# Moving the scale and bias of eight layer norms from GpSimd to VectorE in a five-layer float32 network

## The chip, the cores and the metric

The kernel runs on one core of a Trainium2 chip. The metric is the device time of one execution in microseconds; the time shown is the median of a few runs. The engines named below are TensorE (PE, with its weight loads as PEld), VectorE (DVE), ScalarE (ACT), GpSimd (POOL) and the DMA queue of SyncE (SP).

## The reference

The input is one sequence of 512 tokens with 1024 features, in float32. It passes through four layers of a first block and one layer of a second. Each layer of the first block is, with a mixer that is differential attention (layers 0 and 3), a gated linear recurrence (1) or window attention (2):

```
h = layer_norm(ALPHA * h + mixer(h), ln_g[i, 0], ln_b[i, 0])
u = square(relu(h @ w_up[i])) @ w_down[i]
h = layer_norm(ALPHA * h + u, ln_g[i, 1], ln_b[i, 1])
h = h + sigmoid(h @ w_ple_gate[i]) * (p[i] @ w_ple[i])

layer_norm(x, g, b) = (x - mean) * rsqrt(var + 1e-5) * g + b     # over the 1024 features
```

So there are eight layer norms, two for each of four layers. The second block has two RMS norms, a mixer and a gated feed-forward part, and a last RMS norm ends the network; the change doesn't touch them.

## The kernel before

The residual `hres` stays on the chip as four token tiles of 128 tokens by 1024 features. Beside it lies its transpose, by feature, as two float32 parts `hTh` and `hTl` (the rounded value and what is left), since every product is made as three passes over such parts (`mm3`, lines 274 to 276: high by high, low by high, high by low). Weights come from memory in halves of 512 KB into three buffers `raw`; ScalarE rounds a half into `wh` (L133), and VectorE subtracts to get `wl` (L134), after which that `raw` buffer is free for the next transfer. There are three buffers each of `wh` and `wl`.

Around each layer norm stands a `boundary`: the last products of the phase before are made token tile by token tile (`tail`), and as soon as two token tiles are complete, the work for that half of the tokens follows. VectorE adds the product bank to `hres` (L584), takes the statistics (L532 to L534) and the inverse root (L343 to L359), and the tile is normalized, one tile of each half by ScalarE (L541) and one by VectorE (L537). Then `transposed` runs over the half in four steps of two feature chunks: TensorE transposes four blocks into a bank (L489), ScalarE applies scale and bias by feature into a scratch tile `e` (L501), VectorE casts it into `hTh` (L507) and subtracts for `hTl` (L508). The products of the next phase read `hTh` and `hTl`.

The residual itself needs the same scale and bias, now along the free axis. They are loaded once for each norm, spread over all partitions, into one buffer `gb` of the pool `a8` (it appears as `a` in the rows). Before the change GpSimd does this in place on each token tile: one multiplication (L546) and one addition (L547) of 128x1024. The readers of the scaled residual come later: after the first norm of a layer it is the first addition in `down` (L586), after two quarters of the feed-forward width have been projected; after the second norm it is `add` in `gate` (L724, L726), once the four banks `acc` of the gate's first half are complete.

After the first norm `ffn` projects three weight tiles by halves of the tokens (`fm` with `split=True`): first all three tiles for tokens 0 to 255, then all three for 256 to 511, so that the second half may come late. Two banks (`psA`) alternate; `evict` empties one by ScalarE (L668), VectorE (L669), ScalarE (L333), VectorE (L334). After the second norm the products of `ple` (which don't need the norm) and then those of `gate` follow, in four banks `psD`.

The order of each engine's queue is set at compile time by a planner: it follows the order in which the program names the instructions, and fills an engine that it believes to be idle with later work that is ready by its own estimate. Each queue is then executed in that order. Only inside the attention and recurrence parts is the order written by hand.

Of the kernel before, what the change touches and what calls it, by code (L numbers as in the profile page):

```python
# [21 lines left out]
NT = S // P  # L22
D = 1024
# [25 lines left out]
def shape_constants():  # L49
    """Arrays that depend on the shapes alone."""  # L50
# [45 lines left out]
def weave(main, fill, rate):  # L96
    """Emit the steps of main with those of fill between them, rate of fill per unit that main yields."""
    due = 0.0
    for n in main:
        due += rate * (1 if n is None else n)  # L100
        while due >= 1:
            due -= 1
            next(fill, None)
    run(fill)


class Weights:
    """A weight tile [128, k, n or 2048 / k], to be loaded as its exact parts hi + lo, by halves of k.

    src: (halves, k, n, perm); halves[z]: [(slice of columns, source [128, k / 2, columns])];  # L110
    perm: how the columns are reordered on the way, as (destination view, source view).
    """
# [24 lines left out]
class Stream:  # L137
    """Jobs (sources, steps of the loaded weight tiles), in order, and the sources of a tail; loaded ahead."""
# [15 lines left out]
    def convert(self, n):  # L154
        """The first n halves, with as many more on their way as there is room for."""
        self.fetch(self.converted + self.RAW)
        for t, z in self.halves[self.converted:n]:
            t.convert(z)
            self.converted += 1
            self.fetch(self.converted + self.RAW)  # L160
# [23 lines left out]
class Net:  # L184
# [18 lines left out]
    # ---------------------------------------------------------------- helpers  # L203
# [31 lines left out]
    def dma2(self, out, in_):  # L235
        """Small loads, out of the way of the weights."""
        self.nc.gpsimd.dma_start(out=out, in_=in_)
# [10 lines left out]
    def cols(self, w, c0):  # L248
        """256 columns of a [1024, n] matrix: [128, 8, 256]."""
        wv = w[:, c0:c0 + 256].rearrange("(k p) n -> p k n", p=P)  # L250
        return [[(self.ALL, wv[:, 4 * z:4 * z + 4])] for z in range(2)], 8, 256, None

    def rows4(self, w, r0, n):
        """512 rows, 512 columns: [128, 4, 512]."""
        wv = w[r0:r0 + 512, n * 512:n * 512 + 512].rearrange("(k p) n -> p k n", p=P)
        return [[(self.ALL, wv[:, 2 * z:2 * z + 2])] for z in range(2)], 4, 512, None

    def rows2(self, w, c0, c1):
        """Two chunks of 128 rows, 1024 columns: [128, 2, 1024]."""
        return [[(self.ALL, w[c * P:c * P + P].rearrange("(k p) n -> p k n", p=P))] for c in (c0, c1)], 2, 1024, None  # L260
# [17 lines left out]
    def mm3s(self, products):  # L278
        """Independent products of the same kind, pass by pass: those on other rows of the array may overlap."""
        mm = self.nc.tensor.matmul  # L280
        for n in range(3):
            for ps, (lh, ll), (rh, rl) in products:
                mm(ps, ll if n == 2 else lh, rl if n == 1 else rh, start=n == 0, stop=n == 2)
# [4 lines left out]
    def fm_steps(self, tiles, evict, split=False, act=None):  # L288
        """Feature-major products: evict(tile index, block, psum [128 features, tokens c], c).

        split: by halves of the tokens, over all the tiles, so that the second half may come late.
        """
# [25 lines left out]
    def tm256_steps(self, w, evict):  # L318
        """Token-major products of a [1024, 256] weight tile: evict(pair of token tiles, psum [128, 2, 256])."""
# [11 lines left out]
    def split_to(self, hi, lo, src):  # L331
        """src (f32) into hi + lo."""
# [3 lines left out]
    def rsqrt(self, v, n, engine=None):  # L336
        """1/sqrt of positive [128, n] values: a first guess from the exponent, a Newton and a Halley step."""
# [24 lines left out]
    def exp_small(self, out, x):  # L362
        """exp(x) = ((1 + tanh(x/16)) / (1 - tanh(x/16)))**8 of a small tile."""
# [11 lines left out]
    # ---------------------------------------------------------------- setup  # L375
# [8 lines left out]
    def columns(self, name, rows):  # L384
        """Vectors as columns: rows of 128 values, transposed on TensorE."""
# [14 lines left out]
    def lambdas(self):  # L400
        """lambda of the differential attention, negated."""
# [17 lines left out]
    def tables(self):  # L419
# [16 lines left out]
        # halved biases and scales of the sigmoids taken as tanh  # L436
# [9 lines left out]
        # sinks, negated and not  # L446
# [4 lines left out]
    def biases(self):  # L451
        """The bias of every relative position by head, reversed and laid out as Toeplitz blocks."""
# [25 lines left out]
    # ---------------------------------------------------------------- norms  # L478
    def transposed(self, src, half, scale=None, bias=None):
        """hT of the two token tiles of a half: x * scale + bias by feature, split."""  # L480
        nc = self.nc
        hs = slice(half * 256, half * 256 + 256)
        for cp in range(NC // 2):
# [22 lines left out]
            if bias is not None:  # L506
                nc.vector.tensor_copy(hi, f)  # L507
                nc.vector.tensor_sub(lo, f, hi.bitcast(F32))  # L508

    def boundary(self, tail, half):  # L510
        """The last products of a phase, by token tile, and what follows each half of the tokens."""
# [5 lines left out]
    def layer_norm(self, tail, i, n):  # L517
        """hres <- LN(hres), hT of it."""
# [25 lines left out]
        for t in range(NT):  # L544
            h = self.hres[:, t]
            nc.gpsimd.tensor_mul(h, h, gb[:, :D])  # L546
            nc.gpsimd.tensor_add(h, h, gb[:, D:])  # L547

    def rms_scale(self, t):
        """[128, 1] 1/rms of a token tile of hres."""  # L550
# [9 lines left out]
    def rms_norm(self, tail, key):  # L560
        """hT of rms_norm(hres) * w; hres stays."""
# [11 lines left out]
    def rehT(self, tail=lambda t: None):  # L573
        """hT of hres as it is."""
# [5 lines left out]
    # ---------------------------------------------------------------- products into hres  # L580
# [7 lines left out]
    def out_steps(self, ws, acts, scale):  # L588
        """hres += act^T (two chunks) @ w rows, of each act with its w; act: [(hi, lo)] * 2 of [128, 512]."""
# [11 lines left out]
    def out_tail(self, ws, acts):  # L601
        """The last two such products, by token tile."""
# [25 lines left out]
    def down(self, w, r0, act, scale):  # L628
        """hres += act^T (8 chunks) @ w[r0:r0+1024]."""
# [25 lines left out]
    # ---------------------------------------------------------------- feed-forward of the first block  # L655
    def ffn(self, i):
# [3 lines left out]
        def up(g):  # L660
# [11 lines left out]
            if g == 0:  # L672
                self.fm([(u, w()) for u, w in todo[:3]], evict, split=True)
                todo = todo[3:]
# [10 lines left out]
    def ple_in(self, i):  # L685
        """p transposed and split."""
# [15 lines left out]
    def ple(self, i, pT):  # L702
        """0.5 * (p @ w_ple), token-major."""
# [12 lines left out]
    def gate(self, i, ple):  # L716
        """hres += sigmoid(h @ w_ple_gate) * ple."""
# [10 lines left out]
        for kk in range(2):  # L728
            w_ = self.load_rows4(w, kk * 512, 0)
            for t in range(NT):  # L730
                self.down_part(acc[t], w_, hT, kk, t, kk == 0, kk == 1)
        for t in range(NT):
# [10 lines left out]
    # ---------------------------------------------------------------- attention layers  # L743
    def qk_evict(self, dst, j, ps, scale, s=slice(0, S)):
        """A projected block into hi (slot j) and lo (slot 2 + j)."""
# [10 lines left out]
    def groups_then_out(self, attend, jobs, counts, rates, out):  # L756
        """Four head groups: each attends beside as many jobs as counts says; their results go into hres.

        jobs: (sources, steps, count of steps), or the groups whose result is to go into hres; the last
        two groups are left to the tail that is returned. out(n): the source of the weights of group n.  # L760
        """
# [18 lines left out]
    def unit_rms(self, po, z=None):  # L780
        """[128, 4] 1/rms over the last axis of po / z, over z and sqrt(128); po [128, 4, 128]."""
# [14 lines left out]
    def settle(self, age=0):  # L796
        """What was put off, age calls ago, to let a chain of small steps run beside other products."""
# [5 lines left out]
    def back(self, po, factor, use):  # L803
        """use((po [128, (4 n), m] * factor [128, 4 n]) transposed in a bank), later."""
# [126 lines left out]
    # ---------------------------------------------------------------- gated linear recurrence (HGRN2)  # L931
    def hgrn(self, i):
        nc, io = self.nc, self.io
        w_in = io["hg_w_in"][0]
        # lower bound of this layer
# [62 lines left out]
        def attend(p, oT):  # L998
# [4 lines left out]
            def start(b):  # L1003
                Q, K, f = (heads[b][:, n] for n in range(3))
                # s == t
# [6 lines left out]
                # the products by block: K decays to the end of its block, Q from the start of its own  # L1012
# [3 lines left out]
            def level(b, lev):  # L1016
                """Pairs of neighbouring blocks of length lev: keys in the first, queries in the second."""
# [85 lines left out]
    # ---------------------------------------------------------------- sliding window attention with sinks  # L1103
    def swa(self, i):
# [17 lines left out]
        def seg(u):  # L1122
            """Columns of heads 2u, 2u + 1 and of 8 + 2u, 9 + 2u, as blocks of one head of each kind."""
# [18 lines left out]
        def attend(u, oT):  # L1142
# [10 lines left out]
            def scores(x, tp):  # L1153
                """Heads 2u + x of both kinds, two token tiles: the exponentials."""
# [84 lines left out]
    # ---------------------------------------------------------------- second block  # L1239
    def rope(self):  # L1240
        """cos and signed sin of the positions, by feature."""
# [18 lines left out]
        for out, quarter in ((R[:, 0], 0.25), (R[:, 1], 0.0)):  # L1260
            # n = round(ang / 2pi + quarter), y = ang - n * 2pi + quarter * 2pi
# [11 lines left out]
    def mixer(self):  # L1273
# [97 lines left out]
        def merge_gate(which, u):  # L1371
            """1 + tanh, twice the sigmoid, of one tile of the gate; here its tanh."""
# [9 lines left out]
        def merge_out(which, u, act, w_o, use):  # L1382
            """y^T = w_o^T @ act of one tile, used as use(chunk, tanh, psum)."""
# [14 lines left out]
        # RG-LRU branch  # L1398
# [32 lines left out]
        def gates(n):  # L1431
            """The weights of a block of the recurrence, kept for it."""
# [6 lines left out]
        def recur(n):  # L1439
# [5 lines left out]
            for b in range(2):  # L1445
# [13 lines left out]
                # a = exp(log_a) = (1 + T) / (1 - T), sqrt(1 - a^2) = 2 sqrt(-T) / (1 - T), T = tanh(log_a / 2);  # L1459
                # 1 / (1 - T) by a Newton step from (1 + exp(log_a)) / 2  # L1460
# [64 lines left out]
    def softplus_neg(self, out, lam):  # L1525
        """softplus(-lam) = max(-lam, 0) + log1p(exp(-|lam|)) of [128, 8]."""
# [133 lines left out]
```

## Time and profile before

| | |
|---|---|
| time of three runs | 3714.79, 3715.89, 3718.94 us (median 3715.89) |
| span of the profiled execution | 3717.7 us |
| TensorE busy | 3585.0 us (96%), 18603 instructions |
| VectorE busy | 2038.4 us (55%) |
| ScalarE busy | 1327.3 us (36%) |
| GpSimd busy | 298.1 us (8%), 448 instructions |

The profiled execution has its span as its own time; it lies among the three runs, 1.8 us above their median. Busy times are shares of the whole span. TensorE's busy time uses modelled ends of matmuls, so the waits that the trace lists for it are the surer reading. An instruction's duration runs from the moment it has been started to its end, including any time in which it was held.

### The profile page before, as it was taken

Reading aid. Unit: us, or ns where it says so; the run is one execution under the profiler, and the core shown is the slowest. Engines: PE = TensorE matmul, PEld = TensorE weight load, DVE = VectorE, ACT = ScalarE, POOL = GpSimd, SP = SyncE. Lnnn points to the kernel's source line nnn. Section 1 sums busy time; section 2 is a strip of 40 time slices with the busy share of each in tenths; the row PEclk is TensorE's granted clock in tenths of the full one; section 3 lists DMA queues with packets and bytes.
Section 4 is the critical chain, followed back from the end, with each engine's and each line's share of the span. In section 5 each row is a group of like instructions: output and inputs, shape, how many; then the busy total and the mean of one; then the engine's idle time right before and its main releaser. Section 6 shows DMA issues by size and latency. Waiting matters only on the chain. (4 is left out here: it accounts for less than half of the span.)

```text
span 3717.7 us, 46654 instructions
## 1 busy us (share of the span) xinstructions
PE 3585.0 (96%) x18603; PEld 2995.6 (81%) x18603; DVE 2038.4 (55%) x3738; ACT 1327.3 (36%) x2201; POOL 298.1 (8%) x448
## 2 busy tenths in 40 slices
PE   7998999999989999999999999899999999999999
PEld 6877888798878887878887888788878888888887
DVE  3566334756674337466335655733476547664444
ACT  3443222322233223544222344322234327534331
POOL 1112000210120002011001111200020001000000
PEclk9999999999989999999999999999999999999999
DMA  5432323212222333123332222233322232323322
GB/s 163 109 97 80 102 91 108 80 57 66 66 86 92 102 114 97 46 69 95 98 94 94 91 86 91 84 92 96 106 91 74 80 102 76 112 91 97 96 91 80
DMA packets 260441, 338.20 MB, mean 91 GB/s; under 512 B 10917, under 2 KB 196652, under 8 KB 260096
## 3 DMA queue, kind: packets, MB, share of 16 engines
q1 hardware_dynamic: 259568, 334.83, 28.9%
q8 instruction: 146, 2.39, 0.3%
q0 software_dynamic: 656, 0.40, 0.1%
q14 instruction: 71, 0.58, 0.1%
HBM read 333.03 MB, written 8.45 MB: 92 GB/s over the span
## 5 line engine op out<-in xcount | busy, mean ns | idle before, releaser
L134 DVE TENSOR_TENSOR wl<-raw,wh 128x1024 fp32r<-128x1024 f32 (+1 forms) x586 | 693.7, 1198 | 676.0 <-ACT wh L133 674.2
L274 PE MATMUL A<-hTh,wh 128*128 128x512 f32 (+1 forms) x2704 | 1007.6, 373 | 34.6 <-DVE k L669 27.8
L275 PE MATMUL A<-hTl,wh 128*128 128x512 f32 (+1 forms) x2704 | 989.0, 366 | 20.2 <-DVE hTl L508 19.9
L276 PE MATMUL A<-hTh,wl 128*128 128x512 f32 (+1 forms) x2704 | 986.8, 365 | 0.0
L133 ACT CAST wh<-raw 128x1024 fp32r<-128x1024 f32 (+1 forms) x586 | 591.3, 1030 | 1003.0 <-PE D L276 438.0
L274 PEld LDWEIGHTS A<-hTh,wh 128*128 128x128 f32 x2704 | 516.6, 191 | 125.7 <-DVE k L669 28.6
L275 PEld LDWEIGHTS A<-hTl,wh 128*128 128x128 f32 x2704 | 516.7, 191 | 103.8 <-DVE hTl L508 21.5
L274 PE MATMUL D<-wh,a 128*128 128x512 f32 x1472 | 581.2, 395 | 19.7 <-DVE hres L584 18.9
L276 PEld LDWEIGHTS A<-hTh,wl 128*128 128x128 f32 x2704 | 515.9, 191 | 88.5
L276 PE MATMUL D<-wh,a 128*128 128x512 f32 x1472 | 577.5, 392 | 0.0
L275 PE MATMUL D<-wl,a 128*128 128x512 f32 x1472 | 577.0, 392 | 0.0
L274 PEld LDWEIGHTS D<-wh,a 128*128 128x128 f32 x1472 | 278.3, 189 | 80.2 <-DVE hres L584 20.6
L276 PEld LDWEIGHTS D<-wh,a 128*128 128x128 f32 x1472 | 278.3, 189 | 57.8
L275 PEld LDWEIGHTS D<-wl,a 128*128 128x128 f32 x1472 | 278.7, 189 | 56.4
L584 DVE TENSOR_TENSOR hres<-D,hres 128x512 f32<-128x512 f32 x212 | 145.7, 688 | 182.6 <-PE D L276 182.5
L546 POOL TENSOR_TENSOR hres<-hres,a 128x1024 f32<-128x1024 f32 x32 | 84.6, 2665 | 1751.4 <-PE T L489 1688.6
L274 PE MATMUL A<-wh,hTh 128*128 128x256 f32 x512 | 151.3, 295 | 2.8 <-DVE k L1287 2.8
L669 DVE SCALAR_TENSOR_TENSOR k<-A,k 128x512 f32<-128x512 f32 (+1 forms) x152 | 91.5, 602 | 104.1 <-ACT k L668 104.1
L333 ACT CAST a<-k 128x512 fp32r<-128x512 f32 (+1 forms) x172 | 94.7, 550 | 146.6 <-DVE k L669 127.7
L276 PE MATMUL A<-wh,hTl 128*128 128x256 f32 x512 | 143.6, 281 | 0.0
L275 PE MATMUL A<-wl,hTh 128*128 128x256 f32 x512 | 143.6, 280 | 0.0
L334 DVE TENSOR_TENSOR a<-k,a 128x512 fp32r<-128x512 f32 (+1 forms) x172 | 107.2, 624 | 53.3 <-ACT a L333 53.2
(307 smaller groups left out, 4070.3 us busy)
## 6 DMA issues: line engine op xcount, KB each, us to landing
raw<-in_w_up_dram SPq DMA_DIRECT2D x128, 512.0 KB, 4.7
raw<-in_w_down_dram SPq DMA_DIRECT2D x128, 512.0 KB, 4.4
raw<-in_w_in_dram SPq DMA_DIRECT2D x56, 512.0 KB, 3.7
raw<-in_da_w_in_dram SPq DMA_DIRECT2D x48, 512.0 KB, 3.6
raw<-in_ffn_w_up_dram SPq DMA_DIRECT2D x48, 512.0 KB, 4.5
raw<-in_w_ple_gate_dram SPq DMA_DIRECT2D x32, 512.0 KB, 4.5
raw<-in_hg_w_in_dram SPq DMA_DIRECT2D x32, 512.0 KB, 3.6
raw<-in_ffn_w_down_dram SPq DMA_DIRECT2D x24, 512.0 KB, 4.6
```

Of the source, the lines that this page charges most:

```text
L133: net.nc.scalar.copy(dst(hv), src(r))
L134: net.nc.vector.tensor_sub(dst(lv), src(r), dst(hv).bitcast(F32))
L274: mm(ps, lh, rh, start=first, stop=False)
L275: mm(ps, lh, rl, start=False, stop=False)
L276: mm(ps, ll, rh, start=False, stop=last)
L333: self.nc.scalar.copy(hi, src)
L334: self.nc.vector.tensor_sub(lo, src, hi.bitcast(F32))
L546: nc.gpsimd.tensor_mul(h, h, gb[:, :D])
L584: self.nc.vector.tensor_add(h, ps, h)
L669: nc.vector.scalar_tensor_tensor(a, in0=ps, scalar=0.0, in1=r, op0=ALU.max, op1=ALU.mult)
```

## The change

`layer_norm` no longer issues L546 and L547. It leaves a function, `affine`, that makes the same eight operations on VectorE. `ffn` calls it after the three tiles that are projected by halves, and `gate` after the products of its first half. The operations are tied to the last `hTl` subtraction of `transposed`: none of them stands ahead of it in VectorE's queue. The diff also takes out comments and docstrings, which issue nothing.

```
             if bias is not None:
                 nc.vector.tensor_copy(hi, f)
-                nc.vector.tensor_sub(lo, f, hi.bitcast(F32))
+                self.last_lo = nc.vector.tensor_sub(lo, f, hi.bitcast(F32))
...
         self.boundary(tail, half)
-        for t in range(NT):
-            h = self.hres[:, t]
-            nc.gpsimd.tensor_mul(h, h, gb[:, :D])
-            nc.gpsimd.tensor_add(h, h, gb[:, D:])
+        after = self.last_lo.ins
+
+        def affine():
+            with self.tc.issue_after(after):
+                for t in range(NT):
+                    h = self.hres[:, t]
+                    nc.vector.tensor_mul(h, h, gb[:, :D])
+                    nc.vector.tensor_add(h, h, gb[:, D:])
+        self.affine = affine
...
             if g == 0:
                 self.fm([(u, w()) for u, w in todo[:3]], evict, split=True)
+                self.affine()
                 todo = todo[3:]
...
                 self.down_part(acc[t], w_, hT, kk, t, kk == 0, kk == 1)
+        self.affine()
         for t in range(NT):
             add(acc[t], t, 0)
```

## Rows read from the trace of the kernel before

**Rows 1.** The page: span, and busy time of each engine

```profile
span 3717.7 us, 46654 instructions
...
PE 3585.0 (96%) x18603; PEld 2995.6 (81%) x18603; DVE 2038.4 (55%) x3738; ACT 1327.3 (36%) x2201; POOL 298.1 (8%) x448
```

**Rows 2.** TensorE's waits over the span: total us, times, longest us

```profile
PE A L274 <- DVE k L669: 27.8, 4, 7.1
PE A L275 <- DVE hTl L508: 19.9, 5, 4.7
PE D L274 <- DVE hres L584: 18.9, 4, 4.7
...
PE T L489 <- ACT hres L541: 7.0, 4, 1.9
PE A L274 <- DVE hTh L507: 6.2, 4, 1.7
...
PE T L489 <- DVE hres L537: 2.2, 6, 0.6
```

**Rows 3.** Timeline of GpSimd, 652 to 666 us: start, duration, instruction

```profile
652.99 5.30 POOL L546 TENSOR_TENSOR hres<-hres,a 128x1024 f32<-128x1024 f32 x2 [339.23 <-PE T L489]
658.26 5.58 POOL L547 TENSOR_TENSOR hres<-hres,a 128x1024 f32<-128x1024 f32 x2
```

**Rows 4.** Timeline of VectorE in the same stretch

```profile
653.02 2.99 DVE L507 CAST hTh<-e 128x512 fp32r<-128x512 f32 x2
655.93 5.71 DVE L508 TENSOR_TENSOR hTl<-e,hTh 128x512 fp32r<-128x512 f32 x2
661.56 2.56 DVE L507 CAST hTh<-e 128x512 fp32r<-128x512 f32 x1
664.04 0.68 DVE L584 TENSOR_TENSOR hres<-D,hres 128x512 f32<-128x512 f32 x1
```

**Rows 5.** L507 over the span: minimum, median, maximum duration in ns

```profile
L507 DVE CAST hTh<-e x64: 375/427/2656, 276.1 to 2760.3; 128x512 fp32r<-128x512 f32 x64
```

**Rows 6.** L508 over the span, the same columns

```profile
L508 DVE TENSOR_TENSOR hTl<-e,hTh x64: 674/694/2915, 276.5 to 2763.0; 128x512 fp32r<-128x512 f32 x64
```

**Rows 7.** A small VectorE operation between 682.5 and 685.5 us, by line

```profile
L953 DVE TENSOR_TENSOR base<-lb,oml 128x8 f32<-128x8 f32 x1 | 2.4, 2383 | 0.0
```

**Rows 8.** Groups of VectorE by line: busy us, mean ns of one | idle before

```profile
L508 DVE TENSOR_TENSOR hTl<-e,hTh 128x512 fp32r<-128x512 f32 x64 | 106.9, 1677 | 0.9
L507 DVE CAST hTh<-e 128x512 fp32r<-128x512 f32 x64 | 89.8, 1409 | 12.5 <-ACT e L501 12.5
```

**Rows 9.** L134 over the span: minimum, median, maximum duration in ns

```profile
L134 DVE TENSOR_TENSOR wl<-raw,wh x586: 680/1220/1229, 12.0 to 3678.9; 128x1024 fp32r<-128x1024 f32 x187, 128x512 fp32r<-128x512 f32 x9
```

**Rows 10.** Thirteen windows after waits: length, busy by engine, PEclk, DMA share, GB/s

```profile
288.20:291.60 3.40, 3.40 (x16) 3.22 (x16) 3.40 (x7) 1.24 (x1) 0.00 (x0) 0.50 0.01 2
...
2739.50:2741.40 1.90, 1.75 (x5) 1.37 (x6) 1.90 (x6) 0.00 (x0) 0.00 (x0) 0.60 0.00 0
sum 45.10, PE 44.12 PEld 39.49 DVE 35.68 ACT 11.72 POOL 1.60; mean PE 3.39 PEld 3.04 DVE 2.74 ACT 0.90 POOL 0.12
```

**Rows 11.** Sum of four 20 us windows behind the last L508, first norms

```profile
sum 80.00, PE 77.55 PEld 77.21 DVE 40.42 ACT 35.99 POOL 0.00; mean PE 19.39 PEld 19.30 DVE 10.10 ACT 9.00 POOL 0.00
```

**Rows 12.** A 10 us window behind the last L508, second norms; columns of rows 10

```profile
691.30:701.30 10.00, 10.00 (x45) 8.19 (x45) 7.23 (x10) 3.30 (x5) 0.00 (x0) 1.00 0.62 205
```

**Rows 13.** Sum of the windows of three boundaries without a norm (rehT)

```profile
sum 63.00, PE 62.87 PEld 53.85 DVE 40.60 ACT 29.84 POOL 0.00; mean PE 20.96 PEld 17.95 DVE 13.53 ACT 9.95 POOL 0.00
```

**Rows 14.** GpSimd's waits over the span: total us, times, longest us

```profile
POOL hres L546 <- PE T L489: 1688.6, 13, 339.2
```

**Rows 15.** The page, DMA issues: count, KB each, us from issue to landing

```profile
raw<-in_w_up_dram SPq DMA_DIRECT2D x128, 512.0 KB, 4.7
```

**Rows 16.** Timeline of VectorE, 325 to 337 us: bank after bank emptied

```profile
325.25 0.42 DVE L669 SCALAR_TENSOR_TENSOR k<-A,k 128x256 f32<-128x256 f32 x1
...
330.90 0.42 DVE L669 SCALAR_TENSOR_TENSOR k<-A,k 128x256 f32<-128x256 f32 x1
```

## Prediction

> **What bounds the kernel now.** I read the page first. TensorE is busy for 3585.0 of 3717.7 us, VectorE for little over half, GpSimd for a twelfth [rows 1]. By shares alone nothing that moves off GpSimd can matter, and a longer VectorE is covered. But 132.7 us of TensorE's span are idle, so the second view is who TensorE waits for. Six of its waits stand at the boundaries of the layer norms, and they come to 27.8 + 19.9 + 18.9 + 7.0 + 6.2 + 2.2 = 82.0 us [rows 2]: for the first bank of the feed-forward part to be emptied (L669), for `hTl` and `hTh`, for the addition to `hres` that frees a bank (L584), and for the normalized tile (L541, L537). Most of these end on VectorE; none ends on GpSimd.
>
> The third view, the timeline of one boundary, shows why VectorE is late. GpSimd's four scale and bias operations of the first token half run from 652.99 to 663.84 [rows 3]. In that same stretch the casts and subtractions into `hTh` and `hTl` take about 2.6 to 2.9 us each, one for each operation of GpSimd, and the addition that TensorE needs comes only at 664.04 [rows 4]. Over the run the same instructions have medians of 0.427 and 0.694 us and maxima of 2.656 and 2.915 [rows 5, 6]. The size of the work is not the reason: an addition of 128x8, beside GpSimd, took 2.383 us [rows 7]. So in this trace a VectorE instruction that meets one of these GpSimd operations is held until that one ends. GpSimd is on the path through VectorE, though no wait names it.
>
> **The change part by part.** Removed: 8 x 8 = 64 operations on GpSimd. With them goes the holding. L507 has a mean of 1.409 us against a median of 0.427, and L508 1.677 against 0.694 [rows 5, 6, 8]: 64 x 0.982 + 64 x 0.983 = 125.8 us, and with 2.2 us of the small addition [rows 7] 128 us of VectorE's time come free, 16 us at each norm.
>
> What that is worth to TensorE is the 82.0 us of waits, at most [rows 2], and the slow restart behind them. In thirteen stretches right behind these waits, together 45.1 us, TensorE is busy for 44.1 us at a granted clock of 0.50 to 0.60 [rows 10]. That is the level of 1.2 GHz, after VectorE kept TensorE idle; taken as half speed it costs some 22 us. Without the waits the clock has no reason to fall there. The potential is 82 + 22 = 104 us.
>
> Not all of it will come. The waits for L541 and L537 (9.2 us) fall where GpSimd is quiet; they are the chain from the last product through statistics and inverse root, late because the addition before it was late. From below, three boundaries without a norm and without GpSimd leave TensorE idle for 0.13 of 63 us [rows 13], but their chain is shorter. From above, all 9.2 us may stay. I take 8 us for all eight norms, near the upper end, since those chains keep their length.
>
> Added: 64 operations of 128x1024 on VectorE. L134 has the same shape and two such inputs: median 1.220 us [rows 9]. Eight are 9.8 us at each norm, 78 us over the run. They can't stand ahead of the last L508, so they delay nothing that the transposes need. What covers them is VectorE's slack behind that point. After the first norms VectorE is busy for 10.1 of 20 us [rows 11]; 9.8 us just fit. After the second norms it is busy for 7.2 of 10 us, one of four such windows, all alike [rows 12], mostly with weight subtractions for the gate's second half. There the additions of `gate` wait for TensorE's 96 products into four banks in any case: 45 take 10 us in that row, so 96 take 21 us. The casts and subtractions of the second half, 4 x (0.43 + 0.69) = 4.5 us [rows 5, 6], and 9.8 us of scale and bias end inside that.
>
> Behind an operation of the new block stand, on VectorE, the emptying of banks (L669, L334) and the weight subtractions (L134); ScalarE's casts and TensorE's next bank wait for those. Banks come 5.65 us apart [rows 16] and there are two, so a block of 9.8 us in one piece could stop TensorE for some 4 us; in pieces it stops nothing. The cost lies between 0 and 78 us (every operation exposed). I take 4 us, one for each first norm, near the lower end, because the slack in the row is as long as the block.
>
> No DMA is moved. `gb` is held until the new operations end, as before until GpSimd's; its load is no issue, for GpSimd's first multiplication is released by TensorE's transposes in thirteen cases [rows 14].
>
> The sum: 104 - 8 - 4 = 92 us. The profiled execution's 3717.7 us becomes 3625.7. The median of the runs shown is 1.8 us below that span, so the forecast is **3624 us**, 2.5% faster.
>
> **The rivals.**
>
> *VectorE bounds the boundaries throughout.* Then what counts is VectorE's own time: 128 us of holding go, 78 us of work come, and the gain is 50 us: 3666 us. For it: VectorE is busy nearly without a break around the norms, and when 14 us of TensorE's waiting vanish, the same work has to fit into a shorter stretch. Against it: TensorE has three weight tiles of the first token half to work on while VectorE ends the second, and the new work stands behind the last L508, where VectorE is half idle [rows 11]. Beside this stands a rule of the Trainium skill: Perfetto Trace Analysis, section Optimizing Scalar/DVE Operations, says that GpSimd and VectorE share a port into SBUF, so that moving work between the two might not help. By that rule the sum would be the 50 us of this rival or less, not 92. The held instructions of this trace agree that the two engines share something; no run here shows yet whether a move is lost. An operation of this shape takes 1.22 us on VectorE against 2.65 on GpSimd [rows 3, 9], so the swap is not even.
>
> *Nothing changes.* The casts could be slow for another reason that only coincides with GpSimd's operations, or TensorE's queue order could hold it elsewhere: 3716 us. Against it: the 128x8 addition [rows 7], and casts at 0.427 us as soon as GpSimd is quiet.
>
> *Slower: the weight ring stalls.* The planner may set all eight operations in one block ahead of the weight subtractions. A `raw` buffer is freed only by L134, so the next transfer starts 9.8 us late and lands 4.7 us after issue [rows 15]: 14.5 us of TensorE waiting at each norm, 116 us in all, against 104 saved: 3716 + 12 = 3728 us. It decides from 104 / 8 = 13 us of exposed wait at each norm. Against it: the program names the weights of the three tiles ahead of the new operations, and three buffers are loaded ahead.
>
> **How the numbers follow.** A measurement of this kernel can tell about 0.2% (7 us) from no change. The forecast has a chance of 0.74, VectorE as the bound 0.18, no change 0.04, the stalled ring 0.04. So faster has 0.92, same 0.04, slower 0.04. Within the forecast the whole potential gives 3716 - 104 = 3612, and if a tenth of the remaining 51 us of idle time goes with it, 3607; with 24 us more of exposed blocks (6 us at each first norm) it is 3648. That is its own range, 3607 to 3648. The other likely case lies at 3666, and somewhat above if the waits shorten less. The range that leaves out less than 2 in 10 is 3603 to 3675.
>
> **What would show it.** In the profile after, no GpSimd instruction lies in a norm; L507 and L508 have maxima near their medians of 0.43 and 0.69; the waits of [rows 2] for L669, L508, L507 and L584 are nearly gone, and the stretches at half clock behind them too. The new operations take about 1.2 us each. TensorE's idle time falls from 133 to some 50 us. The prediction is wrong if new waits for L669, `wl` or `hres` appear behind the norms, if the new operations take much longer than L134, or if the second half's chain (L537, L541) keeps TensorE waiting for as long as the casts did.

## The result, and the profile after

The changed kernel takes 3613.06 us (median of four runs, 3612.09 to 3615.10), against 3717.41 us before in the same session (four runs): a ratio of 0.9719, with a 95% interval of 0.9707 to 0.9730. That is 104 us less. The forecast was 3624 us; the range of 3603 to 3675 holds the result.

The profiled execution after has a span of 3610.0 us, 107.7 us less than before. (Its time is 3612.09 us: the span leaves out 2.1 us. The table of before takes the span, 3717.7 us, for that execution's time. With some 2 us more it would be the fourth run of before, 3719.75 us; the median of the four, 3717.41 us, lies beside the span and not 1.8 us below it.) The page gives the span and the busy time of each engine, to be read against [rows 1]:

```profile
span 3610.0 us, 46577 instructions
...
PE 3553.7 (98%) x18603; PEld 2970.9 (82%) x18603; DVE 1972.3 (55%) x3802; ACT 1328.6 (37%) x2201; POOL 130.3 (4%) x384
```

TensorE executes the same 18603 matmuls. Its idle time falls from 132.7 to 56.3 us, and its busy time from 3585.0 to 3553.7 us: of 107.7 us, 76.4 are waiting that went and 31.3 are matmuls that run faster. VectorE does 64 more instructions and is nevertheless busy for 66 us less. The mean granted clock of TensorE over the span rises from 0.986 to 0.997.

TensorE's waits after (total us, times, longest us), the lines that answer to [rows 2]:

```profile
PE T L489 <- DVE hres L537: 3.2, 7, 0.6
PE A L274 <- DVE k L674: 2.6, 4, 1.0
```

The waits for `hTl`, `hTh`, the addition that frees a bank, and ScalarE's normalized tile no longer have a line at the norms. What stays is the wait for VectorE's normalized tile (L537), 3.2 us where 2.2 were, and 2.6 us for the first bank of the feed-forward part (L674 here, L669 before), where 27.8 were.

VectorE's instructions over the span (minimum, median, maximum in ns): first the cast and the subtraction of [rows 5, 6], then the new multiplication.

```profile
L507 DVE CAST hTh<-e x64: 376/420/428, 275.5 to 2647.3; 128x512 fp32r<-128x512 f32 x64
...
L508 DVE TENSOR_TENSOR hTl<-e,hTh x64: 673/687/695, 276.0 to 2647.7; 128x512 fp32r<-128x512 f32 x64
...
L550 DVE TENSOR_TENSOR hres<-hres,a x32: 1209/1216/1223, 297.1 to 2654.0; 128x1024 f32<-128x1024 f32 x32
```

Not one cast or subtraction is held any more: the maxima are 0.428 and 0.695 us where they were 2.656 and 2.915. Where the new operations stand shows in VectorE's timeline behind the first norm:

```profile
295.79 0.68 DVE L508 TENSOR_TENSOR hTl<-e,hTh 128x512 fp32r<-128x512 f32 x1
296.39 0.41 DVE L334 TENSOR_TENSOR a<-k,a 128x256 fp32r<-128x256 f32 x1
296.72 0.41 DVE L674 SCALAR_TENSOR_TENSOR k<-A,k 128x256 f32<-128x256 f32 x1
297.06 1.21 DVE L550 TENSOR_TENSOR hres<-hres,a 128x1024 f32<-128x1024 f32 x1
298.19 0.41 DVE L334 TENSOR_TENSOR a<-k,a 128x256 fp32r<-128x256 f32 x1
298.53 1.21 DVE L551 TENSOR_TENSOR hres<-hres,a 128x1024 f32<-128x1024 f32 x1
```

They come between the steps that empty a bank, not as one block: one at a time at first, and once three in a row (303.27 to 306.75 us). The last of the first norm's eight ends at 308.2 us, and VectorE has no idle time at all between 302.9 and 312.9 us, while TensorE is busy throughout.

Windows of 50 us over the norms (length, busy time and instructions of each engine, granted clock, DMA share, GB/s); the first, the second, and the sum of eight:

```profile
276.00:326.00 50.00, 48.66 (x364) 45.13 (x363) 42.34 (x77) 26.36 (x50) 0.00 (x0) 1.00 0.34 106
633.00:683.00 50.00, 49.48 (x229) 40.24 (x229) 43.91 (x86) 25.00 (x39) 0.00 (x0) 1.00 0.34 106
...
sum 400.00, PE 393.87 PEld 341.96 DVE 340.38 ACT 208.49 POOL 0.00; mean PE 49.23 PEld 42.75 DVE 42.55 ACT 26.06 POOL 0.00
```

The granted clock is 1.00 in all eight, so the stretches at half clock of [rows 10] are gone. TensorE is idle for 6.1 of 400 us at the norms. VectorE is now busy for 85% of them.

### The profile page after: what moved, and what is told of

It is laid out like the page before. It is cut to its first block, busy times and chain, and to the rows that moved or that the text cites. A ratio compares the mean times of both kernels' runs of the same rounds, so it can differ in the third digit from the quotient of the medians.

```text
span 3610.0 us, 46577 instructions
## 1 busy us (share of the span) xinstructions
PE 3553.7 (98%) x18603; PEld 2970.9 (82%) x18603; DVE 1972.3 (55%) x3802; ACT 1328.6 (37%) x2201; POOL 130.3 (4%) x384
## 4 chain that ended last, share of the span: by engine, by line
PE 82%; DVE 9%; ACT 4%; DMA 3%; issue 2%; POOL 1%; SPq 0%; DVEq 0%; ACTq 0%; POOLq 0%
PE A L274 15%; PE A L276 15%; PE A L275 15%; PE D L276 10%; PE D L275 10%; PE D L274 10%; PE D L283 1%; PE D L1035 1%; DVE wl L134 1%; ACT wh L133 1%; PE T L489 1%; PE D L901 1%; DMA raw<-in_w_up_dram 1%; DVE hres L589 1%; DVE hTl L508 1%
## 5 line engine op out<-in xcount | busy, mean ns | idle before, releaser
L134 DVE TENSOR_TENSOR wl<-raw,wh 128x1024 fp32r<-128x1024 f32 (+1 forms) x586 | 693.4, 1198 | 650.0 <-ACT wh L133 648.1
L274 PEld LDWEIGHTS A<-hTh,wh 128*128 128x128 f32 x2704 | 508.5, 188 | 94.2 <-issue 6.2
L276 PEld LDWEIGHTS A<-hTh,wl 128*128 128x128 f32 x2704 | 508.1, 188 | 88.4
L275 PEld LDWEIGHTS A<-hTl,wh 128*128 128x128 f32 x2704 | 509.1, 188 | 81.8 <-issue 1.7
L674 DVE SCALAR_TENSOR_TENSOR k<-A,k 128x512 f32<-128x512 f32 (+1 forms) x152 | 91.4, 601 | 96.8 <-ACT k L673 96.5
L673 ACT ACTIVATE k<-A 128x512 f32<-128x512 f32 (+1 forms) x152 | 80.0, 526 | 135.9 <-PE A L276 135.9
```

The source lines that it names most:

```text
L134: net.nc.vector.tensor_sub(dst(lv), src(r), dst(hv).bitcast(F32))
L274: mm(ps, lh, rh, start=first, stop=False)
L275: mm(ps, lh, rl, start=False, stop=False)
L276: mm(ps, ll, rh, start=False, stop=last)
L673: nc.scalar.activation(r, ps, AF.Relu)
L674: nc.vector.scalar_tensor_tensor(a, in0=ps, scalar=0.0, in1=r, op0=ALU.max, op1=ALU.mult)
```

## The experiments

Ratios are against the kernel before, measured beside each run; intervals are 95%.

**The engine undone, the place kept.** GpSimd makes the eight operations, released by the last L508.

```diff
-            with self.tc.issue_after(after):
-                for t in range(NT):
-                    h = self.hres[:, t]
-                    nc.vector.tensor_mul(h, h, gb[:, :D])
-                    nc.vector.tensor_add(h, h, gb[:, D:])
...
+            for t in range(NT):
+                h = self.hres[:, t]
+                for op, k in ((nc.gpsimd.tensor_mul, 0), (nc.gpsimd.tensor_add, D)):
+                    x = op(h, h, gb[:, k:k + D])
+                    self.tc.add_manual_dep(x.ins, after.name, behind, reason="late")
```

> The eight operations stay on GpSimd but are released only by the last hTl subtraction, so the place of the change is kept and the engine undone. If holding VectorE is the cause and it costs only where casts stand beside it, the casts are free again, the emptying of banks and the weight subtractions behind the norms are held instead (21 us of GpSimd at each norm), and the additions of the gate come some 3 to 5 us late: 3620 to 3660 us. If the place alone made the gain: 3613. If holding costs the same wherever GpSimd runs: 3690 to 3717.

Measured: 3637.37 us, ratio 0.9787 (0.9772 to 0.9801), so 24 us above the changed kernel. The casts are free (L507 at most 0.428 us). The lateness has moved behind the norms, as the timeline of VectorE beside GpSimd's operations shows, where line 675 is VectorE's first step in emptying a bank:

```profile
297.34 1.77 DVE L334 TENSOR_TENSOR a<-k,a 128x256 fp32r<-128x256 f32 x1 [0.47 <-ACT a L333]
299.03 0.41 DVE L675 SCALAR_TENSOR_TENSOR k<-A,k 128x256 f32<-128x256 f32 x1
...
304.69 2.87 DVE L134 TENSOR_TENSOR wl<-raw,wh 128x1024 fp32r<-128x1024 f32 x1 [0.49 <-ACT wh L133]
307.48 0.41 DVE L675 SCALAR_TENSOR_TENSOR k<-A,k 128x256 f32<-128x256 f32 x1
307.81 3.06 DVE L134 TENSOR_TENSOR wl<-raw,wh 128x1024 fp32r<-128x1024 f32 x1
```

Each subtraction of two SBUF tensors that meets GpSimd is held (0.42 becomes 1.77, 1.22 becomes 3.06 in these rows), while L675, which reads one of its operands from PSUM, stays at 0.41. TensorE waits 4.6 to 4.9 us for a bank at each first norm. So three quarters of the gain (79 of 104 us) come from taking the work out from between the casts, and 24 us more from taking it off GpSimd.

**The place undone, the engine kept.** The eight operations on VectorE are named right behind the boundary, as GpSimd's were, with no tie to the last L508.

```diff
-        after = self.last_lo.ins
-        def affine():
-            with self.tc.issue_after(after):
+        for t in range(NT):
+            h = self.hres[:, t]
+            nc.vector.tensor_mul(h, h, gb[:, :D])
+            nc.vector.tensor_add(h, h, gb[:, D:])
...
```

> VectorE, but named right behind the boundary and not tied to the last hTl subtraction: the four operations of the first token half (4.9 us) may stand between the two halves. If the engine is what matters and the place is a detail, 3613 to 3620. If the tie is needed, the chain of the second half comes up to 4.9 us later at each norm, covered by TensorE's first-half tiles at the first norms and exposed at the four second norms: 3625 to 3640.

Measured: 3643.74 us, ratio 0.9802 (0.9788 to 0.9817): 31 us above the changed kernel. The tie is needed, but I had the wrong norms and the wrong chain of work. TensorE's waits (as above):

```profile
PE A L274 <- DVE k L669: 12.9, 4, 3.7
PE A L276 <- DVE sm L350: 10.8, 4, 2.7
...
PE T L489 <- DVE hres L537: 0.2, 1, 0.2
```

VectorE's timeline between the two halves of the first norm, where L546 and L547 are the new operations, and the product that waits:

```profile
282.01 1.21 DVE L546 TENSOR_TENSOR hres<-hres,a 128x1024 f32<-128x1024 f32 x1
283.14 0.20 DVE L533 BATCH_NORM_AGGREGATE sm<-st 128x2 f32<-128x12 f32 x1
283.26 1.17 DVE L546 TENSOR_TENSOR hres<-hres,a 128x1024 f32<-128x1024 f32 x1
284.35 0.15 DVE L534 TENSOR_SCALAR sm<-sm 128x1 f32<-128x1 f32 x1
...
286.87 1.22 DVE L134 TENSOR_TENSOR wl<-raw,wh 128x1024 fp32r<-128x1024 f32 x1
```

```profile
288.15 0.38 PE L276 MATMUL A<-hTh,wl 128*128 128x256 f32 x1 [2.73 <-DVE sm L350]
```

The same stretch in the changed kernel:

```profile
282.04 1.21 DVE L134 TENSOR_TENSOR wl<-raw,wh 128x1024 fp32r<-128x1024 f32 x1
283.16 0.20 DVE L533 BATCH_NORM_AGGREGATE sm<-st 128x2 f32<-128x12 f32 x1
283.28 1.17 DVE L134 TENSOR_TENSOR wl<-raw,wh 128x1024 fp32r<-128x1024 f32 x1
```

The small steps (L533, L534) stand behind operations of 1.2 us in both kernels, at the same times, so they don't make the difference. What is late is the weights: the four operations of the first half stand where the changed kernel makes three weight subtractions, and the first of these moves from 282.04 to 286.87. The product that waits reads `wl`. It starts at 288.15, when that subtraction has just ended (288.09); the list names L350, a small step that ends at 288.15 and that this product doesn't read. Behind the second half a bank comes late in the same way: three more of the operations stand between 300.98 and 304.81, with one step that empties a bank among them, and the next such step starts only at 305.06. The chain of the second half is some 2.4 us later than in the changed kernel (L537 at 291.77 against 289.42), but TensorE's waits for L537 are 0.2 us over the whole span, and there is no line for L541 or L508. All eight waits fall at the four first norms (four of 2.6 to 2.7 and four of 3.1 to 3.7 us), not at the second norms: there TensorE still has the `ple` products to make.

**No scale and bias at all.** `affine` does nothing.

> Scale and bias of the residual are left out altogether (its values are then not the reference's). If the block on VectorE is hidden, 3609 to 3613, the time of the changed kernel or a few us less. If VectorE's own time counts at the norms, the 78 us of the new work show: 3613 less 30 to 78 us.

Measured: 3607.40 us, ratio 0.9704 (0.9688 to 0.9720), just under the lower end of what I expected. Of the 78 us of work that the change adds to VectorE, 5.7 us show in the time. The intervals of the two ratios overlap, but the slowest of the four runs (3608.98) lies below the fastest of the changed kernel (3612.09).

**The first norms alone, and the second norms alone.** The others keep GpSimd at its old place.

```diff
+        if not (n == 0):        # the other run: n == 1
+            for t in range(NT):
+                h = self.hres[:, t]
+                nc.gpsimd.tensor_mul(h, h, gb[:, :D])
+                nc.gpsimd.tensor_add(h, h, gb[:, D:])
+            self.affine = lambda: None
+            return
```

> Only the four first norms of a layer go to VectorE; the four second norms keep GpSimd at its old place. By the waits listed for TensorE before, the first norms hold 54 of the 82 us and some 17 of the 22 us at half clock, so 33 us of the gain are missing: 3646 us. If the gain is not additive by norm (the planner's order as a whole made it), far from that: below 3630 or above 3665.

> The complement: only the four second norms go to VectorE. If the gain is additive by norm, some 71 of 104 us are missing: 3684 us, and the gains of this run and of the one with the first norms add up to 104. If not, their sum is far from it.

Measured: 3648.17 us, ratio 0.9814 (0.9800 to 0.9829), with the first norms alone; 3681.94 us, ratio 0.9905 (0.9891 to 0.9918), with the second norms alone. The two gains, 1.86% and 0.95%, add up to the 2.81% of the whole. Each run keeps the waits of the norms it left alone. With the first norms alone:

```profile
PE D L274 <- DVE hres L596: 18.8, 4, 4.7
```

and with the second norms alone (L681 empties a bank):

```profile
PE A L274 <- DVE k L681: 27.9, 4, 7.1
PE A L275 <- DVE hTl L508: 19.9, 5, 4.7
```

These are the rows of before to within 0.1 us [rows 2].

**The block doubled.** Each operation is made twice.

```diff
-                for t in range(NT):
+                for t in [t for t in range(NT) for _ in range(2)]:
```

> The changed kernel with each of the eight operations made twice (scale and bias are applied twice, so the values are not the reference's): 9.8 us more on VectorE at each norm. If the block of the change lies in slack that it nearly fills, part of the second block is exposed, some 3 us at each second norm and 3 to 8 us at each first norm: 3635 to 3660. If VectorE had no slack at all, 78 us: 3691. If the slack is much longer than the block, 3613.

Measured: 3663.76 us, ratio 0.9853 (0.9840 to 0.9867): 51 us above the changed kernel, somewhat over the top of what I expected. The first 78 us of work cost 5.7 us, the second 78 cost 51. TensorE's waits, and the sum of four windows of 20 us behind the first norms (busy us by engine):

```profile
PE A L274 <- DVE k L674: 12.0, 4, 3.4
PE D L275 <- DVE wl L134: 11.9, 5, 3.7
PE A L276 <- DVE wl L134: 10.9, 4, 3.0
```

```profile
sum 80.00, PE 65.86 PEld 62.13 DVE 79.52 ACT 30.44 POOL 0.00; mean PE 16.47 PEld 15.53 DVE 19.88 ACT 7.61 POOL 0.00
```

VectorE is busy for 79.5 of 80 us there: the block of the change fills the slack, and most of what is added beyond it (51 of 78 us) comes out, as late banks and late weights and as matmuls at a lower clock: the granted clock is 0.93 and 0.84 in the first two of these windows, and TensorE is busy for 3571.6 us over the span, 17.9 more than in the changed kernel.

**What GpSimd holds, by what it does.** In the kernel before, GpSimd's operations are replaced by memsets, which read nothing, and in another run by operations with one input. One execution each.

```diff
-            nc.gpsimd.tensor_mul(h, h, gb[:, :D])
-            nc.gpsimd.tensor_add(h, h, gb[:, D:])
+            for _ in range(4):
+                nc.gpsimd.memset(h, 1.0)
# the other run:
+            for _ in range(2):
+                nc.gpsimd.tensor_scalar(h, in0=h, scalar1=1.0, scalar2=0.0, op0=ALU.mult, op1=ALU.add)
```

> The kernel before, with GpSimd's eight operations at each norm replaced by four memsets of each residual tile, which read nothing from SBUF (the residual is then a constant, not the reference's). If GpSimd holds VectorE by what it reads, the subtraction L508, which has two SBUF inputs, is free at 0.69 us; the cast L507 is free too unless writes alone can hold it. If any work of GpSimd on these tiles holds any VectorE instruction, both stay as long as one memset.

> The kernel before, with GpSimd's multiplication and addition at each norm replaced by two operations with a single SBUF input each (times one, plus zero: scale and bias of the residual are left out). If what GpSimd reads holds the subtraction L508, which reads two SBUF tensors, it is held again, with maxima over 1.2 us, where memsets left it at 0.69. If only a two-input GpSimd operation holds it, L508 stays at 0.69 and only the cast L507 is held.

With memsets (128 of 1.03 us), 3636.84 us; cast and subtraction over the span:

```profile
L507 DVE CAST hTh<-e x64: 417/531/5364, 274.7 to 2673.8; 128x512 fp32r<-128x512 f32 x64
...
L508 DVE TENSOR_TENSOR hTl<-e,hTh x64: 672/688/696, 275.1 to 2674.3; 128x512 fp32r<-128x512 f32 x64
```

With one input (64 of 1.31 us), 3647.94 us:

```profile
L507 DVE CAST hTh<-e x64: 411/427/1283, 275.3 to 2686.1; 128x512 fp32r<-128x512 f32 x64
...
L508 DVE TENSOR_TENSOR hTl<-e,hTh x64: 672/695/1528, 275.8 to 2687.4; 128x512 fp32r<-128x512 f32 x64
```

Memsets never hold the subtraction (at most 0.696 us) and hold the cast. A GpSimd operation that reads one tensor and writes one holds both. So the subtraction is held by what GpSimd reads, and not by its writes alone. The cast is held by operations that only write; whether reading alone would hold it no run shows, since every operation tried here writes.

**More of the same.** The other GpSimd operations of some size are the multiplication by the sine of the rotary embedding and one in the recurrence of the second block; both go to VectorE. In a second version the first norms' block is also named after the fourth weight tile.

```diff
-                nc.gpsimd.tensor_tensor(sw, sw, R[:, 1, s], op=ALU.mult)
+                nc.vector.tensor_tensor(sw, sw, R[:, 1, s], op=ALU.mult)
...
-                nc.gpsimd.tensor_mul(tr, tr, r)
+                nc.vector.tensor_mul(tr, tr, r)
# the second version also:
                 self.fm([(u, w()) for u, w in todo[:3]], evict, split=True)
-                self.affine()
...
         up(0)
+        self.affine()
```

> The changed kernel, with the last large GpSimd operations moved too: the multiplication by the sine of the rotary embedding (12 of 1.0 us) and the one of the recurrence (8 of 2.2 us) go to VectorE. If holding costs only where VectorE stands in TensorE's way, there is little left: 3608 to 3613, at most the 2.5 us that TensorE waits behind the rotary addition. If each us of GpSimd beside VectorE costs, 20 to 30 us less.

> The kernel of the last look (the multiplications of the rotary embedding and of the recurrence on VectorE too), with the first norms' eight operations named only after the fourth weight tile, so that its weights and the emptying of its banks come ahead of them in the planner's order. If the 3.5 to 4 us that TensorE still waits for the first bank behind the first norms come from the block, they go: 3602 to 3605 us. If the planner fills VectorE's idle time with the block as before, no change: 3607.

Measured: 3606.89 us, ratio 0.9703 (0.9690 to 0.9716), and 3603.87 us, ratio 0.9694 (0.9681 to 0.9708). The first is slightly better than I expected, the second as expected. In the second, TensorE's waits have no line for L674 at the norms any more, and the chain of the second half is what remains:

```profile
PE T L489 <- DVE hres L537: 4.2, 7, 1.3
```

The second version is 9 us (0.25%) below the changed kernel by the medians. Its slowest of five runs (3605.28) lies below the fastest of the changed kernel (3612.09), though the intervals of the two ratios touch.

## Why the prediction was right

*GpSimd on the path through VectorE.* Shown. L507 and L508 have the maxima that were forecast, the waits went, and the run that keeps GpSimd but puts it behind the casts frees the casts and holds what stands there instead. Beside this the Trainium skill, SBUF — State Buffer, section Who interferes with whom, says that a cast in a 2-port mode contends with GpSimd in general, and an operation with two SBUF inputs contends with what GpSimd reads. The two runs with memsets and with one input agree, with 0.696 and 1.528 us as the subtraction's maximum and 5.364 and 1.283 us as the cast's; no run here shows which mode the cast is in. Only the prediction's sentence that any VectorE instruction that meets these operations is held was too wide. A step with one operand in PSUM is not held: the addition L584 in the trace before, beside L547 of GpSimd, and L675 above (0.41 us). GpSimd, then VectorE:

```profile
282.58 4.82 POOL L547 TENSOR_TENSOR hres<-hres,a 128x1024 f32<-128x1024 f32 x2
```

```profile
285.04 0.68 DVE L584 TENSOR_TENSOR hres<-D,hres 128x512 f32<-128x512 f32 x1
```

*The potential of 104 us.* The mechanism was right, the sizes of two terms were off. TensorE's waits were given as 82, less 8 that would stay and less 4 for new ones: 70. Measured are 76.4 us of idle time: the chain leaves 3.2 us for L537 and nothing for L541, where I took 8, near the upper bound. I chose that end because the chain keeps its length; but the lower bound, the boundaries with no norm, was the nearer row, because the chain was late only through the addition before it. (The sum leaves 133 - 70 = 63 us of idle time, the list of signs says some 50; 56.3 were left.)

*The restart at half clock.* Sized at 22 us from thirteen windows; TensorE's busy time fell by 31.3. The clock is 1.00 at all norms now. The thirteen windows were too short. Taken over the whole stretches that the profile of before records at half clock around the norms, thirteen too, TensorE is busy for 54.5 us:

```profile
sum 81.90, PE 54.51 PEld 48.45 DVE 68.06 ACT 16.75 POOL 19.62; mean PE 4.19 PEld 3.73 DVE 5.24 ACT 1.29 POOL 1.51
```

Taken as half speed again, that is some 27 us. The other 4 us are not located; TensorE's modelled ends leave an uncertainty of their own.

*The cover for the new work.* Taken at 4 us, measured 5.7 (the run without scale and bias). One reading under it was wrong: banks don't come 5.65 us apart. Between the two lines of [rows 16] stand others, and a bank is emptied at 325.25, 327.05, 330.90 and 332.70 us. So 5.65 us is the time of two banks, which is also what the 4 us for a block in one piece need (9.8 less 5.65). The statement that the block just fits is what the doubled block shows. The prediction left open whether it comes in pieces: at the first norms it does, between the steps that empty a bank; behind the second norms it is one piece of 9 us (655.1 to 664.3 at the first of them), and TensorE waits for none of it.

*The rivals.* VectorE as the bound of the boundaries (50 us of gain) falls: the first block costs 5.7 of 78 us. It is what the kernel meets with a little more work, as the doubled block shows, and with the work in the wrong place. The rule from Perfetto Trace Analysis in the Trainium skill, that moving work between the two engines might not help, didn't hold here: the same work in the same place is 24 us faster on VectorE. No change is excluded by the result, and the stalled weight ring by its absence: none of the waits after ends on a `raw` transfer at the norms.

## What to carry to other kernels

An engine that no wait of TensorE's names at a stage can still be on the critical path, through an engine that it holds: compare an instruction's maximum with its median, and look at what runs beside the slow ones. Work that nobody needs soon belongs behind the last instruction that somebody waits for, on whichever engine, and weights and banks count as much as the chain itself; here place was worth 31 us with the engine right, and the engine 24 us with the place right. And slack is a length: a block that fits costs little (6 of 78 us), the next one of the same size costs most of what it takes (51 of 78).

## What the runs showed of the hardware

A held cast can be held by several operations in a row. With memsets, the cast at 2650.93 us of that trace took 4.54 us, beside a row of memsets of about 0.95 us each, while two subtractions just before it ran at their normal length. VectorE and GpSimd in that stretch:

```profile
2649.73 1.27 DVE L508 TENSOR_TENSOR hTl<-e,hTh 128x512 fp32r<-128x512 f32 x2
2650.93 4.54 DVE L507 CAST hTh<-e 128x512 fp32r<-128x512 f32 x1
2655.39 0.67 DVE L584 TENSOR_TENSOR hres<-D,hres 128x512 f32<-128x512 f32 x1
```

```profile
2649.47 5.72 POOL L547 MEMSET hres<- 128x1024 f32 x6
```

So a cast doesn't always get its turn after one GpSimd operation; in the kernel before, beside operations of 2.65 us on average, no cast took longer than 2.656 us. Why, no run here shows.
